# First Q and K in full precision from unsplit weights, x split once with its sums in place, two gate pairs interleaved, weight sums as additions

## The chip, the core and the metric

The kernel runs on one core of one Trainium2 chip. The metric is the device time of one execution in microseconds (us): 1400.05 before, the median of three runs (1399.22 to 1400.08). TensorE (PE) multiplies matrices and adds into PSUM; VectorE (DVE), ScalarE (ACT) and GpSimd (POOL) work on tiles; SyncE (SP) issues most transfers.

## What is computed

One hybrid layer in fp32 for 512 tokens of width 2048: an RMS norm, one input projection, three attention branches of four heads of 128 columns, merge gates, and an output projection with the residual.

```python
hn = rmsnorm(x, norm_g)
proj = jnp.einsum('bsd,dc->bsc', hn, w_in)
br = proj[..., :QKVG_COLS].reshape(b, s, N_BRANCH, 4, BRANCH_W)       # q, k, v, g
f_logit = proj[..., QKVG_COLS:QKVG_COLS + N_HEADS] + b_f
gates = jax.nn.sigmoid(proj[..., QKVG_COLS + N_HEADS:] + b_gate).reshape(b, s, N_BRANCH, D_MODEL)
...
ys = ys * jax.nn.silu(br[:, :, :, 3])
up = jnp.einsum('bsnw,nwd->bsnd', ys, w_up)
merged = jnp.sum(gates * up, axis=2)
return x + jnp.einsum('bsd,de->bse', merged, w_out)
```

## The kernel before

Branch A is an attention with forget gates (four logits per token, the "four heads' logits"), B a chunked one with a learned bias, C a stick-breaking one. The kernel takes the branches in the order C, B, A, four heads each, then the up projections with the merge gates, then the output projection.

**Three products for one.** A factor in fp32 is split into a high and a low part of type fp32r: ACT rounds the high part (`split_to`, L92), VectorE subtracts it from the tile for the low part (L93). `mm3` multiplies high by high, low by high and high by low (L101 to L103), so one matmul is three rows. Weights arrive as raw tiles of 512 KB (`load`, L138: six slots), and are split into `wh` and `wl` (three slots each). x lies transposed, 16 k tiles of 128 by 512 tokens, multiplied by the norm's gain; `rstd`, the norm's factor of each token, is known only after the sums of squares (`norm_x`, L247) and `rsqrt` (L235 to L240).

**Pairs.** `pair_task` computes two column tiles of 128 with seven products in place of eight (Strassen's scheme in Winograd's form): a product has 24 rows of 256 tokens. It needs sums of the weights' four blocks (raw tiles added on VectorE: L315, L324, L325, L327) and of x (`combos`: x by gain and rstd on VectorE, L255, four sums on GpSimd, L257 to L260, and their splits). The results come together in three tiles u, c1, c2 (`after_of`). Both gate pairs that follow the first head, all heads but the first, the other gates and the output projection go by pairs. The first head's Q, K, V and G (`first_head`) go by whole columns (`col_task`, 512 tokens, two units of 24 rows), from x without rstd, which is multiplied in as they leave PSUM (`scaled`, L626); x is split then (`prep_x`), and again after the norm for the pairs (`parts1`, `parts2`).

**The order.** The work is a list of units of up to 24 matmul rows. The emission at the end of the program splits the weights of a unit three units ahead and loads them seven ahead; `at` hangs further work, such as the stages of a head's attention (`stick_scores`, `stick_sums` L548, `soft_scores`, `av`), on a later unit by the numbers in `OFF`. For the first `OFF["man"]` units PE keeps the order of the code; from then on a scheduler orders each engine's instructions when the program is built. PSUM has four banks `acc` for products and four `att` for all else.

## Time and profile before

| what | value |
| --- | --- |
| runs, median of three | 1400.05 us (1399.22 to 1400.08) |
| profiled execution: span | 1397.6 us |
| PE busy, share of the span | 98% |
| VectorE, ACT, GpSimd busy | 85%, 52%, 4% |
| transfers, mean | 126 GB/s |

The profile is of one execution; its span lies 2.45 us under the median of the runs. In a line of the timeline stand the start, the length, the engine, the line of the kernel, the tile written and the tiles read, and in brackets the idle time ahead with what ended it. Matmul rows overlap, so what one costs is the distance of two starts, not its length.

### The profile page before, as it was taken

How to read it: one execution, taken by the hardware profiler on the slowest of the kernel's cores; microseconds unless marked ns; L12 is line 12 of the kernel's file. 1: busy time of each engine (PE TensorE's matmuls, PEld its weight loads, DVE VectorE, ACT ScalarE, POOL GpSimd, SP SyncE). 2: the span in 40 equal slices, each digit the busy share in tenths (PEclk: the TensorE clock that was granted, in tenths of full speed). 3: DMA queues.
4: the chain of work that ended last, by engine and by line, in shares of the span. 5: the costliest groups of instructions: out<-in, count | busy, mean ns of one | idle time of the engine just before them, and what ended most of it. 6: DMA issues, size and time to landing. Idle time of an engine off the chain costs nothing.

```text
span 1397.6 us, 25474 instructions
## 1 busy us (share of the span) xinstructions
PE 1366.3 (98%) x10452; PEld 1316.7 (94%) x10452; DVE 1191.8 (85%) x1671; ACT 729.7 (52%) x1042; POOL 53.7 (4%) x60
## 2 busy tenths in 40 slices
PE   6969999999999999999999999999999999999999
PEld 3759999999999999999999999999999988899999
DVE  8999898887978889888888888888888888898886
ACT  6345564544545555555556555545555755453332
POOL 4730000000000000000000000000000000000000
PEclk9989999999999999999999999999999999999999
DMA  7113334323344244342433333333233766535542
GB/s 272 46 46 106 122 102 126 121 91 114 106 129 126 95 114 128 113 129 95 117 122 115 121 94 119 113 114 121 91 115 103 273 197 203 169 109 176 164 151 76
DMA packets 63093, 176.39 MB, mean 126 GB/s; under 512 B 7400, under 2 KB 9320, under 8 KB 62976
## 3 DMA queue, kind: packets, MB, share of 16 engines
q1 hardware_dynamic: 59520, 170.49, 38.4%
q10 hardware_dynamic: 3456, 4.26, 0.8%
q8 instruction: 82, 1.34, 0.4%
q14 instruction: 35, 0.29, 0.1%
HBM read 155.04 MB, written 19.69 MB: 125 GB/s over the span
## 4 chain that ended last, share of the span: by engine, by line
PE 92%; DVE 5%; issue 1%; ACT 0%; POOL 0%; DMA 0%; SPq 0%; DVEq 0%; ACTq 0%; POOLq 0%
PE acc L101 27%; PE acc L103 27%; PE acc L102 27%; PE att L103 3%; PE att L101 3%; PE att L102 3%; DVE x L255 1%; DVE wl L93 1%; PE att L548 1%; PE att L517 1%; PE att L570 1%; DVE x1l L93 1%; PE att L571 1%; PE att L569 1%; DVE t23l L93 0%
## 5 line engine op out<-in xcount | busy, mean ns | idle before, releaser
L92 ACT ACTIVATE wh<-raw 128x1024 fp32r<-128x1024 f32 (+1 forms) x418 | 435.7, 1043 | 549.2 <-PE acc L102 488.2
L93 DVE TENSOR_TENSOR wl<-raw,wh 128x1024 fp32r<-128x1024 f32 (+1 forms) x418 | 503.9, 1206 | 96.7 <-ACT wh L92 95.9
L102 PE MATMUL acc<-x1l,wh 128*128 128x256 f32 (+1 forms) x768 | 222.3, 289 | 10.5 <-DVE x1l L93 10.5
L103 PE MATMUL acc<-x1h,wl 128*128 128x256 f32 (+1 forms) x768 | 222.0, 289 | 2.2 <-DVE wl L93 2.2
L101 PE MATMUL acc<-x1h,wh 128*128 128x256 f32 (+1 forms) x768 | 223.7, 291 | 0.0
L101 PE MATMUL acc<-x2h,wh 128*128 128x256 f32 (+1 forms) x768 | 223.6, 291 | 0.0
L102 PE MATMUL acc<-x2l,wh 128*128 128x256 f32 (+1 forms) x768 | 221.9, 289 | 0.9 <-DVE x2l L93 0.9
L103 PE MATMUL acc<-x2h,wl 128*128 128x256 f32 (+1 forms) x768 | 221.8, 289 | 0.0
L101 PE MATMUL acc<-t23h,wh 128*128 128x256 f32 x736 | 209.7, 285 | 0.0
L103 PE MATMUL acc<-t23h,wl 128*128 128x256 f32 x736 | 208.4, 284 | 0.0
L102 PE MATMUL acc<-t23l,wh 128*128 128x256 f32 x736 | 208.1, 283 | 0.0
L102 PEld LDWEIGHTS acc<-x1l,wh 128*128 128x128 f32 x768 | 147.8, 192 | 13.4 <-DVE x1l L93 11.2
L103 PEld LDWEIGHTS acc<-x1h,wl 128*128 128x128 f32 x768 | 147.8, 193 | 3.9 <-DVE wl L93 2.4
L102 PEld LDWEIGHTS acc<-x2l,wh 128*128 128x128 f32 x768 | 148.0, 193 | 2.4 <-DVE x2l L93 1.1
L101 PEld LDWEIGHTS acc<-x1h,wh 128*128 128x128 f32 x768 | 147.9, 193 | 1.8 <-issue 0.2
L101 PEld LDWEIGHTS acc<-x2h,wh 128*128 128x128 f32 x768 | 148.2, 193 | 1.3
L103 PEld LDWEIGHTS acc<-x2h,wl 128*128 128x128 f32 x768 | 148.0, 193 | 1.3
L101 PEld LDWEIGHTS acc<-t23h,wh 128*128 128x128 f32 x736 | 141.0, 192 | 0.5
L102 PEld LDWEIGHTS acc<-t23l,wh 128*128 128x128 f32 x736 | 141.0, 192 | 0.1
L103 PEld LDWEIGHTS acc<-t23h,wl 128*128 128x128 f32 x736 | 140.7, 191 | 0.3
L101 PE MATMUL acc<-t,wh 128*128 128x256 f32 x368 | 105.1, 286 | 0.0
L102 PE MATMUL acc<-t,wh 128*128 128x256 f32 x368 | 104.4, 284 | 0.0
(256 smaller groups left out, 2728.0 us busy)
## 6 DMA issues: line engine op xcount, KB each, us to landing
raw<-in_w_col SPq DMA_DIRECT2D x192, 512.0 KB, 3.6
raw<-in_w_out SPq DMA_DIRECT2D x32, 512.0 KB, 3.8
gl<-c SPq DMA_DIRECT2D x48, 256.0 KB, 2.0
raw<-in_w_up SPq DMA_DIRECT2D x32, 384.0 KB, 3.2
sg<-gl SPq DMA_DIRECT2D x48, 256.0 KB, 5.0
x<-in_xT SPq DMA_DIRECT2D x16, 256.0 KB, 5.4
xr<-in_xT SPq DMA_DIRECT2D x16, 256.0 KB, 4.4
yd<-y SPq DMA_DIRECT2D x11, 256.0 KB, 2.0
```

Of the source, the lines that this page charges most:

```text
L92: nc.scalar.activation(hi, src, AF.Copy)
L93: nc.vector.tensor_sub(lo, src, f(hi))
L101: nc.tensor.matmul(ps, lh, rh, start=start, stop=False)
L102: nc.tensor.matmul(ps, lh, rl, start=False, stop=False)
L103: nc.tensor.matmul(ps, ll, rh, start=False, stop=stop)
L255: nc.vector.scalar_tensor_tensor(x, x, gn[:, kt:kt + 1], rstd[0], op0=ALU.mult, op1=ALU.mult)
L517: nc.tensor.transpose(ps[:, blk(i)], st["p"][i][:, blk(j)], identf)
L548: nc.tensor.matmul(ps[:, i * P:], nu_r if i == j else nones_r, part, start=i == j and part is st["lk"][j][0], stop=False)
L569: nc.tensor.matmul(o, vh[:, blk(j)], st["h"][j], start=j == 0, stop=False)
L570: nc.tensor.matmul(o, vl[:, blk(j)], st["h"][j], start=False, stop=False)
L571: nc.tensor.matmul(o, vh[:, blk(j)], st["l"][j], start=False, stop=j == QB - 1)
```

## The change

The first head's Q and K are computed by `first_pair`: 32 fp32 matmuls of the raw weights with x, which ACT multiplies by its gain in place; the norm's sums stand after k tile 9. Then x is multiplied by rstd in place and split once (`split_x`), and V and G go by that; they leave PSUM as copies on ACT (`kept`). The sums of x are made in place on VectorE (`combos`), and their signs turned, which turns signs in `after_of` and `merged_combos`. The four heads' logits follow V and G. The two gate pairs behind them are `late`: their units alternate, one of each pair, and their weight sums are made by transfers that GpSimd issues and that add to the tile (`load_of`). The same holds for the first pair of the output projection, without alternation. In all other pairs VectorE adds, product 5 comes first, and product 3 is added into product 5's bank of PSUM (`more`), to which the last line of `mms_of` belongs. Lines of after lie some ten below or above those of before: the splits are still L92 and L93, the rows of `mm3` L102 to L104.

```diff
-    def mm3(ps, lh, ll, rh, rl, start, stop):
-        nc.tensor.matmul(ps, lh, rh, start=start, stop=False)
-        nc.tensor.matmul(ps, lh, rl, start=False, stop=False)
-        nc.tensor.matmul(ps, ll, rh, start=False, stop=stop)
+    def mm3(ps, lh, ll, rh, rl, start, stop, more=False):
+        nc.tensor.matmul(ps, lh, rh, start=start, stop=False, skip_group_check=more)
+        nc.tensor.matmul(ps, lh, rl, start=False, stop=False, skip_group_check=more)
+        nc.tensor.matmul(ps, ll, rh, start=False, stop=stop, skip_group_check=more)
...
     def prep_x(kt):
         x = xraw[kt]
-        h, lo = xs[kt]
-        if kt % 2:
-            nc.vector.tensor_scalar_mul(h, x, gn[:, kt:kt + 1])
-        else:
-            nc.scalar.activation(h, x, AF.Copy, scale=gn[:, kt:kt + 1])
-        nc.vector.scalar_tensor_tensor(lo, x, gn[:, kt:kt + 1], f(h), op0=ALU.mult, op1=ALU.subtract)
-        s = sqp[kt // 2 % 2] if kt % 2 and kt > 1 else t2("sq")
+        s = t2("sq")
         nc.scalar.activation(s, x, AF.Square)
+        nc.scalar.activation(x, x, AF.Copy, scale=gn[:, kt:kt + 1])
         if kt < 2:
             ssq[kt] = s
         else:
-            (nc.gpsimd, nc.vector)[kt % 2].tensor_add(ssq[kt % 2], ssq[kt % 2], s)
+            nc.vector.tensor_add(ssq[kt % 2], ssq[kt % 2], s)
...
+    def split_x(kt):
+        nc.vector.tensor_mul(xraw[kt], xraw[kt], rstd[0])
+        split_to(*xs[kt], xraw[kt])
     def combos(k):
         a, b = xraw[k], xraw[k + UK]
-        for x, kt in ((a, k), (b, k + UK)):
-            nc.vector.scalar_tensor_tensor(x, x, gn[:, kt:kt + 1], rstd[0], op0=ALU.mult, op1=ALU.mult)
-        t, u = t2("t23"), t2("t4")
-        nc.gpsimd.tensor_sub(t[:, RH], b[:, RH], a[:, RH])
-        nc.gpsimd.tensor_sub(a[:, RH], a[:, RH], a[:, LH])
-        nc.gpsimd.tensor_sub(t[:, LH], b[:, RH], a[:, RH])
-        nc.gpsimd.tensor_sub(u[:, LH], t[:, LH], b[:, LH])
-        split_to(*t23[k], t)
-        split_to(t4[k][:, LH], t4[k][:, RH], u[:, LH])
+        nc.vector.tensor_sub(a[:, LH], a[:, LH], a[:, RH])
+        nc.vector.tensor_sub(a[:, RH], b[:, RH], a[:, RH])
+        nc.vector.tensor_add(b[:, RH], b[:, RH], a[:, LH])
+        nc.vector.tensor_sub(b[:, LH], b[:, RH], b[:, LH])
+    def split_t1(k):
+        (h, lo), a = x1[k], xraw[k]
+        split_to(h[:, RH], lo[:, RH], a[:, LH])
+    def split_t(k):
+        (h, lo), a, b = t23[k], xraw[k], xraw[k + UK]
+        split_to(h[:, LH], lo[:, LH], b[:, RH])
+        split_to(h[:, RH], lo[:, RH], a[:, RH])
+        split_to(t4[k][:, LH], t4[k][:, RH], b[:, LH])
...
-        order = (1, 2, 5, 3, 6, 7, 4) if late else (1, 2, 6, 7, 4, 5, 3)
+        order = (1, 2, 3, 5, 6, 7, 4) if late else (5, 1, 2, 6, 7, 4, 3)
+        (a11, a12), (a21, a22) = src1, src2
+        parts = {1: [a11], 2: [a12], 4: [a22], 5: [a21, a22], 7: [a11, a21], 6: [a21, a22, a11],
+                 3: [a21, a22, a11, a12]}
+        def load_of(i):
+            def go(u):
+                if late:
+                    p = order[i]
+                    w[p] = raw_tile()
+                    nc.sync.dma_start(w[p], parts[p][0])
+                    for src in parts[p][1:]:
+                        nc.gpsimd.dma_start(w[p], src, accum_op=ALU.add)
+                elif i == 0:
+                    for p, src in ((7, a21), (4, a22), (1, a11), (2, a12)):
+                        w[p] = raw_tile()
+                        nc.sync.dma_start(w[p], src)
+            return go
         def prep_of(i):
             p = order[i]
             def go(u):
-                if i == 0:
-                    w[1], a21, w[4], w[2] = kept
-                    split_to(u.hi, u.lo, w[1])
+                if not late and p == 5:
                     w[5] = raw_tile()
-                    nc.vector.tensor_add(w[5], a21, w[4])
-                    if late:
-                        nc.vector.tensor_sub(a21, w[1], a21)
-                        nc.vector.tensor_sub(w[1], w[5], w[1])
-                    w[7], w[6], w[3] = a21, w[1], w[2]
-                    return
+                    nc.vector.tensor_add(w[5], w[7], w[4])
                 split_to(u.hi, u.lo, w[p])
-                if i == 1:
-                    if not late:
-                        nc.vector.tensor_sub(w[7], w[1], w[7])
-                        nc.vector.tensor_sub(w[6], w[5], w[1])
-                if i == (1 if late else 4):
-                    nc.vector.tensor_sub(w[3], w[3], w[6])
+                if not late and p == 1:
+                    w[6] = w[5]
+                    nc.vector.tensor_add(w[7], w[7], w[1])
+                    nc.vector.tensor_add(w[6], w[6], w[1])
+                elif not late and p == 6:
+                    w[3] = w[6]
+                    nc.vector.tensor_add(w[3], w[3], w[2])
             return go
         def mms_of(i):
+            p = order[i]
             def go(u):
-                st["ps"] = ps = acc()[:, LH]
+                more = p == 3 and not late
+                st[p] = ps = st[5] if more else acc()[:, LH]
                 for j in range(UK):
-                    mm3(ps, u.hi[:, j, :], u.lo[:, j, :], *ops[order[i]](j), j == 0, j == UK - 1)
+                    mm3(ps, u.hi[:, j, :], u.lo[:, j, :], *ops[p](j), j == 0 and not more, j == UK - 1, more)
...
-                    add(u[:, LH], u[:, LH], ps)
+                    sub(u[:, LH], ps, u[:, LH])
                     if late:
-                        add(c1[:, RH], c1[:, RH], u[:, LH])
+                        sub(c1[:, RH], c1[:, RH], u[:, LH])
                 elif p == 7:
-                    add(u[:, RH], u[:, LH], ps)
-                    if late:
-                        add(c2[:, RH], c2[:, RH], u[:, RH])
+                    sub(u[:, RH], u[:, LH], ps)
+                    sub(c2[:, RH], u[:, RH], c2[:, RH] if late else st[5])
                 elif p == 4:
                     sub(c2[:, LH], u[:, RH], ps)
                 elif p == 5 and late:
                     nc.scalar.activation(c2[:, RH], ps, AF.Copy)
-                elif p == 5:
-                    add(c2[:, RH], u[:, RH], ps)
-                    add(u[:, LH], u[:, LH], ps)
-                elif late:
-                    add(c1[:, RH], c2[:, RH], ps)
-                else:
-                    add(c1[:, RH], u[:, LH], ps)
+                    add(c1[:, RH], c1[:, RH], ps)
+                elif p == 3 and late:
+                    nc.scalar.activation(c1[:, RH], ps, AF.Copy)
+                elif p == 3:
+                    sub(c1[:, RH], ps, u[:, LH])
...
-    def scaled(st, r):
+    def first_pair(st, n, h):
+        cols = {r: col(n, r, h) for r in (Q, K)}
+        raw = {}
+        ps = {r: Lazy(acc) for r in cols}
+        def load(u):
+            def w(r, i, a, b):
+                if (r, i) not in raw:
+                    raw[r, i] = raw_tile()
+                nc.sync.dma_start(raw[r, i][:, a:b, :], cols[r][i][:, a:b, :])
+            h4 = UK // 2
+            load_x(0)
+            w(Q, 0, 0, h4)
+            w(K, 0, 0, h4)
+            for kt in range(1, UK):
+                load_x(kt)
+            w(Q, 0, h4, UK)
+            w(K, 0, h4, UK)
+            for kt in range(UK, KT):
+                load_x(kt)
+            for r in cols:
+                w(r, 1, 0, UK)
+        def mms(u):
+            for kt in range(KT):
+                for r in cols:
+                    nc.tensor.matmul(ps[r](), raw[r, kt // UK][:, kt % UK, :], xraw[kt],
+                                     start=kt == 0, stop=kt == KT - 1)
+                if kt == OFF["ssq"]:
+                    with tc.high_priority():
+                        norm_x()
+        def after():
+            for kt in range(KT):
+                split_x(kt)
+            for r in cols:
+                st[r] = t2("c")
+                nc.vector.tensor_mul(st[r], ps[r](), rstd[0])
+        return Unit(None, None, mms, load=load, after=after)
+    def kept(st, r):
         def evac(ps):
             st[r] = t2("c")
-            nc.vector.tensor_mul(st[r], ps, rstd[0])
+            nc.scalar.activation(st[r], ps, AF.Copy)
         return evac
     def first_head(n, h):
         st = {}
         fu, fps = f_units()
-        c = {r: col_task(col(n, r, h), xs, scaled(st, r)) for r in (Q, K, V, G)}
-        units.extend([fu[0], c[Q][0], c[K][0], fu[1], c[Q][1], c[K][1],
-                      c[V][0], c[G][0], c[V][1], c[G][1]])
-        def norm_first():
-            with tc.high_priority():
-                norm_x()
-        at(1, norm_first)
-        for k in range(UK):
-            at(OFF["c0"] + k // OFF["c1"], lambda k=k: combos(k))
+        c = {r: col_task(col(n, r, h), xs, kept(st, r)) for r in (V, G)}
+        units.extend([first_pair(st, n, h), c[V][0], c[G][0], c[V][1], c[G][1], fu[0], fu[1]])
+        pairs = []
+        for _ in range(2):
+            u0 = len(units)
+            gate_units(late=True)
+            pairs.append(units[u0:])
+            del units[u0:]
+        units.extend(u for two in zip(*pairs) for u in two)
+        def sums():
+            for k in range(UK):
+                combos(k)
         def parts1():
             for k in range(UK):
-                split_to(*x1[k], xraw[k])
+                split_t1(k)
         def parts2():
             for k in range(UK):
-                split_to(*x2[k], xraw[k + UK])
+                split_t(k)
+        def forget():
             v = t2("f")[:2 * NH, :]
-            nc.vector.tensor_mul(v, fps[:2 * NH, :], rstd[0][:2 * NH, :])
+            nc.scalar.activation(v, fps[:2 * NH, :], AF.Copy)
             nc.sync.dma_start(fd, v)
-            at(12, forget_bias)
-        at(7, parts1)
-        at(9, parts2)
+            at(OFF["fb"], forget_bias)
+        at(OFF["tf"], sums)
+        at(5, parts1)
+        at(6, forget)
+        at(7, parts2)
...
-        gate_units(late=OFF["l1"])
-        gate_units(late=OFF["l2"])
...
-    prep_to(1)
-    load_to(2)
-    for kt in range(4, 8):
-        load_x(kt)
-    load_to(3)
-    for kt in range(8, KT):
-        load_x(kt)
-    for kt in range(UK):
+    load_to(1)
+    for kt in range(KT):
         prep_x(kt)
-    prep_to(2)
-    for kt in range(UK, KT):
-        prep_x(kt)
-        if kt == 11:
-            prep_to(3)
+    load_to(4)
...
-OFF = dict(cs=4, ct=12, nk=5, nq=4, s=12, t=16, v=1, av=8, a0=11, b0=18, c0=3, c1=2, man=17, last=3, l1=0, l2=0)
+OFF = dict(tf=2, cs=4, ct=12, nk=5, nq=4, s=12, t=16, v=1, av=8, ssq=9, fb=10, a0=8, b0=15, man=14, last=3)
```

**GpSimd, in the gate pairs.** Before, its rows are the sums of x, four for each of eight k tiles (t23 and t4 are the sums' tiles); two k tiles:

```order
L257 TENSOR_TENSOR t23_109_427<-x_71_213,x_1_81 128x256
L258 TENSOR_TENSOR x_1_81<-x_1_81 128x256
L259 TENSOR_TENSOR t23_109_427<-x_71_213,x_1_81 128x256
L260 TENSOR_TENSOR t4_110_428<-t23_109_427,x_71_213 128x256
L257 TENSOR_TENSOR t23_111_439<-x_72_215,x_2_83 128x256
L258 TENSOR_TENSOR x_2_83<-x_2_83 128x256
```

After, its rows there are the adding transfers; the last number of a tile tells the product (566 is product 3 of the first pair, 607 of the second; 635 and 719 product 5, 763 and 806 product 6, 862 and 895 product 7):

```order
L322 DMA raw_126_566<-in_w_col 128x1024 x3
L322 DMA raw_129_607<-in_w_col 128x1024 x2
L322 DMA raw_133_635<-in_w_col 128x1024
L322 DMA raw_129_607<-in_w_col 128x1024
L322 DMA raw_140_719<-in_w_col 128x1024
L322 DMA raw_151_763<-in_w_col 128x1024 x2
L322 DMA raw_164_806<-in_w_col 128x1024
L322 DMA raw_168_862<-in_w_col 128x1024
L322 DMA raw_164_806<-in_w_col 128x1024
L322 DMA raw_172_895<-in_w_col 128x1024
```

The sums of x have gone to VectorE, and GpSimd's queue holds ten groups of transfers, in which one tile's transfers stand apart (607, 806).

**VectorE, behind the norm.** Before, the rows behind rstd are the 16 products with gain and rstd, L255; the splits of x by the norm follow later. After, L231 makes rstd, and 13 scalings of k tiles of x (x_59 to x_73) follow it; the last two of them, and what stands behind:

```order
L244 TENSOR_TENSOR x_72_219<-x_72_219,rstd_106_338 128x512
L244 TENSOR_TENSOR x_73_221<-x_73_221,rstd_106_338 128x512
L93 TENSOR_TENSOR x1l_11_138<-x_59_191,x1h_10_137 128x512
L93 TENSOR_TENSOR x1l_13_140<-x_62_197,x1h_12_139 128x512
L93 TENSOR_TENSOR x1l_15_142<-x_63_199,x1h_14_141 128x512
L244 TENSOR_TENSOR x_74_223<-x_74_223,rstd_106_338 128x512
L93 TENSOR_TENSOR x1l_17_144<-x_64_201,x1h_16_143 128x512
```

The first low part now stands behind 13 of the 16 scalings.

**ACT, at the sums of a stick-breaking head (the second of branch C).** Before, between the last exponent of lk and the next evacuation:

```order
L535 ACTIVATE lk_326_1897<-lk_326_1897 128x512
L92 ACTIVATE wh_345_2011<-raw_318_1818 128x1024
L92 ACTIVATE lkh_291_1654<-lk_321_1852 128x384
L92 ACTIVATE lkh_290_1653<-lk_326_1897 128x512
L347 ACTIVATE u_330_1934<-acc_329_1909 128x256
L92 ACTIVATE wh_348_2041<-raw_301_1669 128x1024
```

After:

```order
L550 ACTIVATE lk_309_1840<-lk_309_1840 128x512
L92 ACTIVATE wh_328_1953<-raw_283_1610 128x1024
L92 ACTIVATE wh_331_1983<-raw_302_1761 128x1024
L92 ACTIVATE lkh_275_1598<-lk_305_1796 128x384
L92 ACTIVATE lkh_274_1597<-lk_309_1840 128x512
L366 ACTIVATE u_313_1877<-acc_324_1897 128x256
```

A second weight split now stands ahead of both splits of lk. On PE the row that reads the last of them comes right behind the end of the unit in acc_330:

```order
L102 MATMUL acc_330_1957<-t23h_40_167,wh_318_1884 128x256
L103 MATMUL acc_330_1957<-t23l_41_168,wh_318_1884 128x256
L104 MATMUL acc_330_1957<-t23h_40_167,wl_319_1885 128x256
L563 MATMUL att_340_2020<-lkh_274_1597,nu_r_97 128x512
```

More of the change, by code (lines that the diff above doesn't have):

```diff
@@ L124, in hybrid_kernel, with __init__ @@
     class Unit:
-        def __init__(self, shape, prep, mms, srcs=(), after=None):
-            self.shape, self.prep, self.mms, self.srcs, self.after = shape, prep, mms, srcs, after
+        def __init__(self, shape, prep, mms, src=None, load=None, after=None):
+            self.shape, self.prep, self.mms, self.src, self.load, self.after = shape, prep, mms, src, load, after
             self.hi = self.lo = None
@@ L134, in load @@
     def load(u):
-        u.raw = []
-        for s, keep in u.srcs:
-            t = raw_tile(u.shape)
-            nc.sync.dma_start(t, s)
-            u.raw.append(t)
-            if keep is not None:
-                keep.append(t)
+        if u.load is not None:
+            u.load(u)
+        elif u.src is not None:
+            u.raw = raw_tile(u.shape)
+            nc.sync.dma_start(u.raw, u.src)
     def prep(u):
-        if u.shape is None:
+        if u.prep is None:
             return
@@ L150, in prep_raw @@
     def prep_raw(u):
-        split_to(u.hi, u.lo, u.raw[0])
-    for kt in range(4):
-        load_x(kt)
+        split_to(u.hi, u.lo, u.raw)
     epsc = cp.tile([P, 1], F32, name="epsc")
@@ L340, in go @@
             def go():
-                ps = st["ps"]
+                ps = st[p]
                 if i == 0:
@@ L373, in after_of @@
             return go
-        src = {0: [(src1[0], kept), (src2[0], kept), (src2[1], kept), (src1[1], kept)]}
-        return [Unit([UK, P], prep_of(i), mms_of(i), srcs=src.get(i, ()), after=after_of(i)) for i in range(7)]
+        return [Unit([UK, P], prep_of(i), mms_of(i), load=load_of(i), after=after_of(i)) for i in range(7)]
     side = {}
@@ L744, in after @@
                 merged_combos(d - UK, last_m[0], m)
-        return [Unit([6, P], prep_raw, mms(i), srcs=[(w_up[d, i], None)], after=after if i == 1 else None)
+        return [Unit([6, P], prep_raw, mms(i), src=w_up[d, i], after=after if i == 1 else None)
                 for i in range(2)]
@@ L759, in merged_combos @@
         nc.vector.tensor_sub(t[:, RH], b[:, RH], a[:, RH])
[L760 to L761 removed]
+        nc.vector.tensor_sub(a[:, RH], a[:, LH], a[:, RH])
+        nc.vector.tensor_add(t[:, LH], b[:, RH], a[:, RH])
         nc.vector.tensor_sub(u, t[:, LH], b[:, LH])
@@ L795, in hybrid_kernel, with rest @@
     for e in range(0, DT, 2):
-        def rest(c1l, c1r, c2, e=e):
-            for c, i, sl in ((c2, 1, slice(0, S)), (c1l, 0, LH), (c1r, 0, RH)):
+        def rest(c1l, v, c2, e=e):
+            for c, i, sl in ((c2, 1, slice(0, S)), (c1l, 0, LH), (v, 0, RH)):
                 if i == 1 or sl is LH:
@@ L800, in rest @@
                     nc.sync.dma_start(r, xT[e + i])
-                nc.vector.tensor_add(c, c, r[:, sl])
+                (nc.vector.tensor_sub if sl is RH else nc.vector.tensor_add)(c, c, r[:, sl])
             nc.scalar.dma_start(out[e + 1], c2)
```

7 lines of the change are left out of this document (1 added, 6 removed).

## The prediction

> **What bounds the kernel now.** I read the engine shares first, then the span cut at the places where TensorE stops, then the neighbourhood of each stop.
>
> ```profile
> span 1397.6 us, 25474 instructions
> PE 1366.3 (98%) x10452; PEld 1316.7 (94%) x10452; DVE 1191.8 (85%) x1671; ACT 729.7 (52%) x1042; POOL 53.7 (4%) x60
> ```
>
> The windows, with each engine's busy time in them:
>
> ```profile
> core 0: us, PE busy (x) PEld busy (x) DVE busy (x) ACT busy (x) POOL busy (x), PEclk, DMA share, GB/s
> 0.00:20.16 20.16, 7.74 (x16) 1.15 (x16) 16.05 (x28) 12.40 (x19) 11.20 (x23) 1.00 0.94 350
> 20.16:25.60 5.44, 5.44 (x13) 4.25 (x14) 5.44 (x8) 4.87 (x8) 2.49 (x2) 1.00 0.64 256
> 25.60:72.07 46.47, 46.47 (x202) 35.88 (x200) 44.17 (x52) 17.59 (x28) 27.44 (x24) 1.00 0.19 58
> 72.07:95.02 22.95, 9.34 (x47) 8.22 (x46) 22.95 (x28) 11.44 (x20) 11.05 (x10) 0.70 0.01 1
> 95.02:1237.00 1141.98, 1141.98 (x8894) 1112.88 (x8895) 972.48 (x1387) 621.12 (x895) 1.51 (x3) 1.00 0.40 125
> 1237.00:1262.00 25.00, 22.98 (x186) 22.17 (x185) 23.77 (x36) 13.91 (x23) 0.00 (x0) 1.00 0.34 110
> ```
>
> TensorE (PE) is full for 1141.98 us on end. It idles in three places only: ahead of 20.16, in 72.07 to 95.02, where VectorE (DVE) is busy all the time, and by 2.02 in 1237 to 1262 (what is left of the end is the last stores). So an edit counts by the matmul rows it adds or takes, and by what it does at those places; VectorE's 85% counts nowhere else unless PE comes to wait for it.
>
> **Q and K in full precision.**
>
> ```profile
> 26.10 0.39 PE L103 MATMUL acc<-x1h,wl 128*128 128x512 f32 x1
> 26.33 0.39 PE L101 MATMUL acc<-x1h,wh 128*128 128x512 f32 x1
> ```
>
> and the first rows of the norm, which are fp32:
>
> ```profile
> 28.37 1.02 PE L247 MATMUL att<-sq,tmpc 128*128 128x512 f32 x2
> ```
>
> Split rows of 512 columns start 0.227 apart. The norm's fp32 matmul takes two rows, 0.43 apart (1.02 less 0.59, the length of one), so 0.86. 32 x 0.86 = 27.5 for 96 x 0.227 = 21.8: **+5.7**.
>
> **The start.**
>
> ```profile
> 20.16 0.59 PE L399 MATMUL att<-x1l,w 128*8 128x512 f32 x1 [3.28 <-DVE x1l L224]
> 20.55 0.63 PE L101 MATMUL acc<-x1h,wh 128*128 128x512 f32 x1
> 20.97 0.63 PE L102 MATMUL acc<-x1l,wh 128*128 128x512 f32 x1
> ```
>
> Those were PE's rows in time order; ACT's first square, and its squares and scalings grouped:
>
> ```profile
> 6.02 0.60 ACT L226 ACTIVATE att<-x 128x512 f32<-128x512 f32 x1 [1.26 <-DMA x<-in_xT]
> L226 ACT ACTIVATE sq<-x x9: 612/612/631, 9.5 to 23.9; 128x512 f32<-128x512 f32 x9
> L223 ACT ACTIVATE x1h<-x,small_in x4: 702/706/722, 4.0 to 11.6; 128x512 fp32r<-128x512 f32 x4
> ```
>
> Dense work begins at 20.16, with 15 rows (3.4 us of work) done: 16.8 lost. After, the first product needs only x0 at its gain, behind four squares on ACT. The fourth square reads x3, which now is the sixth 256 KB transfer, not the fourth: at 350 GB/s 0.75 later each, so about 7.5; a square and a scaling (0.61, 0.71) make 8.9: **-7.9**. Rows start 0.42 apart for the first 5.4 us here; I take the same loss for the new start.
>
> **The norm and the split of x.**
>
> ```profile
> 30.47 0.69 ACT L235 ACTIVATE rt<-att,epsc 128x512 f32<-128x512 f32 x1 [0.46 <-PE att L247]
> 34.61 0.69 DVE L240 SCALAR_TENSOR_TENSOR rstd<-rw,rt 128x512 f32<-128x512 f32 x1
> 91.02 1.87 DVE L93 TENSOR_TENSOR x2l<-x,x2h 128x512 fp32r<-128x512 f32 x3
> 188.06 1.06 ACT L92 ACTIVATE wh<-raw 128x1024 fp32r<-128x1024 f32 x1
> 93.16 1.21 DVE L93 TENSOR_TENSOR wl<-raw,wh 128x1024 fp32r<-128x1024 f32 x1
> ```
>
> In ACT's new order three weight splits stand among the last five squares; their load, behind 6.3 MB at 350 GB/s, lands near 22. From there 3 splits, 3 squares and 4 scalings, then VectorE's low part (1.2) and two sums, end near 31.9; PE reaches the norm rows after k tile 9 at 8.9 + 2.7 + 20 x 0.86 = 28.8, and waits about 3.2. The rows end at 33.7; rstd takes from about 30.4 to 35.3 in the rows above, 4.9, so it is there at 38.6. PE has 12 fp32 matmuls left and comes to V at 44.0. VectorE's order is 13 scalings by rstd, then eight low parts, with three scalings and one eviction among them: (1.87 - 0.67) / 2 = 0.60 each, 25 x 0.61 = 15.3. V's first half needs them one by one and ends at 54.2 rather than 44.0 + 24 x 0.227 = 49.4: 4.8. Together **+8.0**; between 0 (squares early, low parts ahead of PE) and 12.8 (the splits' load 4.8 later, by the slowest landing below).
>
> **The gap at 72 to 95.**
>
> ```profile
> 74.65 0.39 PE L103 MATMUL acc<-x1h,wl 128*128 128x256 f32 x1 [2.19 <-DVE wl L93]
> 81.47 0.58 PE L102 MATMUL acc<-x1l,wh 128*128 128x256 f32 x1 [4.18 <-DVE x1l L93]
> 88.75 0.58 PE L102 MATMUL acc<-x1l,wh 128*128 128x256 f32 x1 [6.27 <-DVE x1l L93]
> 95.24 0.28 PE L103 MATMUL acc<-x2h,wl 128*128 128x256 f32 x1
> 95.36 0.28 PE L101 MATMUL acc<-t23h,wh 128*128 128x256 f32 x1
> ```
>
> VectorE's low parts beside GpSimd (54 to 84; busy, mean ns) and then without it (least, median, most ns):
>
> ```profile
> L93 DVE TENSOR_TENSOR x1l<-x,x1h 128x512 fp32r<-128x512 f32 x7 | 8.2, 1221 | 0.0
> ```
>
> ```profile
> L93 DVE TENSOR_TENSOR x2l<-x,x2h x8: 670/674/683, 84.1 to 94.3; 128x512 fp32r<-128x512 f32 x8
> ```
>
> PE waits for the second split of x, which VectorE does late: beside GpSimd's sums (busy 27.44 and 11.05 in the two windows) a low part takes 1.22, without them 0.67. After, x is split once, the sums stand on VectorE at its free pace, the four heads' logits and both gate pairs' products that need no sums lie ahead of those that do. The 47 rows there need 47 x 0.12 = 5.6: 22.95 - 5.6, **-17.3**. What is late next is the sums T2, T3, T4, due only with product 6; I expect them in time.
>
> **Stick-breaking heads.**
>
> ```profile
> 189.07 1.05 ACT L92 ACTIVATE lkh<-lk 128x384 fp32r<-128x384 f32 x2
> ...
> 190.94 1.06 ACT L92 ACTIVATE wh<-raw 128x1024 fp32r<-128x1024 f32 x1 [0.55 <-PE acc L102]
> ```
>
> Before, the weight split that awaits the end of a unit (last row) stands behind the splits of lk that the sums on PE read. After, in heads 1 to 3 of branch C, it stands ahead of two of them, and the next PE row is the sum that reads them. The weight split's slot comes free only as that unit ends, so PE waits 1.06 + 1.05 = 2.1, three times: **+6.2**. Low end 0, if the unit ends earlier than ACT comes to it.
>
> **Accumulating transfers.** 21 weight sums are added by transfers issued on GpSimd, 14 in the gate pairs, 7 in the first output pair. No row of before has such a transfer; the nearest is the plain 512 KB load:
>
> ```profile
> raw<-in_w_col SPq DMA_DIRECT2D x192, 512.0 KB, 3.6
> ```
>
> ```profile
> L138 SPq DMA_DIRECT2D raw<-in_w_col x192: 327/328/780, 2.7 to 1060.8; - x192
> ...
> DMA to landing us min/median/max: 2.8/3.6/8.4
> ```
>
> GpSimd takes them in order and each needs the one before on its tile. Product 3 of the second pair gets its slot when G's second half is split, so its plain load lands near 67. From there five links follow in series to the second product 6 (two of product 3, two of product 6 and the load or sum between), with three issues by GpSimd among them, which I put at 0.6 to 1 each, an estimate from the 0.33 to 0.78 that SyncE's issues of the same tiles take. PE wants that product at 54.2 + 3 x 5.45 (V, G) + 7.3 (logits, 32 rows of 0.227) + 9 x 2.88 (products of 24 rows of 0.12) + 1.0 of narrow starts = 104.8, its split 1.2 earlier. So the chain is late if a link exceeds (103.6 - 67 - 3) / 5 = 6.7. Ends: 2.8, a plain load's least, and 10.5, the slowest plain load with a quarter on top. A sum reads its source and the tile it adds to, twice what a load reads: 2 x 3.6 = 7.2; the slowest load was 8.4, and 7.8 stands between. I take it: 5 x 1.1 = **+5.5**. The first output pair has three such links in series to its product:
>
> ```profile
> 1239.05 0.38 PE L101 MATMUL acc<-m2h,wh 128*128 128x256 f32 x1 [0.37 <-ACT wh L92]
> ...
> 1240.31 0.39 PE L103 MATMUL acc<-m2h,wl 128*128 128x256 f32 x1 [0.76 <-DVE wl L93]
> ```
>
> 3 x 1.1 = **+3.3**, beside the waits that stand there already. Each us on a link is worth 8.
>
> At nothing I cost the copies of V and G on ACT (52% busy), the turned signs, and two weight sums fewer on VectorE per pair where it has slack; if that cover failed, a copy would cost 0.6, four heads' worth 2.4. Adding product 3 into product 5's bank makes PE wait for VectorE's read of that bank after product 7; product 4's 24 rows (2.88) stand between and hide one read of 0.4.
>
> **Sum.** 5.7 - 7.9 + 8.0 - 17.3 + 6.2 + 5.5 + 3.3 = +3.5. The profiled execution's span is 1397.6, the median of the runs shown 1400.05, 2.45 more. So 1401.1 + 2.45, **1403.6**. What a measurement of this kernel can tell from no change is 0.2%, so the same is 1397.25 to 1402.85.
>
> **Rivals.** (a) The other side, **faster**: a link lands in 7.0 or less. At 6.7 the 5.5 and 3.3 are gone, and it is 1394.7, 5.3 under before. For it: the median load of 3.6, and the transfer engines at share 0.19 and 0.01 from 25.6 to 95. Against: a sum is two reads and a write, in series, from an engine that issues none now. At 8 us for each us of link a gain ends at 6.7 + 5.3 / 8 = 7.4, and one that can be measured (2.8) at 7.0. The Trainium skill, "DMA: Bandwidth & Descriptors", section "Anatomy of one DMA — SWDGE (gpsimd) path", fits GpSimd's transfers as 2.0 us and bytes at 436 GB/s, 3.2 here, by which this rival would hold; no run here shows it, and the plain load from SyncE took 3.6.
>
> (b) **Links of 10.5** or more: 2.7 more on eight, 1425.
>
> (c) **VectorE holds up GpSimd's issues.** The rows of 1.22 against 0.67 show the two in each other's way. If each link loses one more such pair (1.2), 8 x 1.2 = +9.6, 1413. Against: the issue moves no data through GpSimd's own datapath that this trace shows. The Trainium skill, "SBUF — State Buffer", section "SBUF: two separate sides", warns that GpSimd cannot write a transfer's descriptors while VectorE runs an operation in a two-port mode, and elsewhere on the page it infers that an addition of two tiles doesn't block that; the slowed rows here are additions of two tiles against GpSimd's arithmetic, so they don't settle it.
>
> (d) **Each pair waits for the bank** by a weight split's length, 50 x 1.2 = 60 more, 1464, if VectorE's queue puts the read behind others; it decides from 2.88.
>
> (e) **No stick-breaking waits:** 6.2 less, 1397.4.
>
> **Chances.** Forecast 0.42 (links of 7.0 to 8.7; own range 1397 to 1411), (a) 0.30, (c) 0.08, (b) 0.09, (e) 0.06, (d) 0.03, and 0.02 for none. Faster: 0.30 of (a), 0.02 of (e), 0.02 for none, 0.34. Same: 0.20 of the forecast, 0.04 of (e), 0.24. Slower: 0.22 of the forecast, (b), (c) and (d), 0.42. Range 1390 to 1426: from (a) with half the norm's term gone, to (b).
>
> **What would show it.** PE's first product near 9; a wait ahead of the norm's rows; waits for x1l up to 54; no idle stretch at 72 to 95; three waits of 2.1 at the stick-breaking sums for lkh; landing times of GpSimd's transfers, and PE waiting for a weight's high part near 105 and 1240. It is wrong if a link takes under 7.0 or over 8.7, if PE waits at each product 3, or if the sums T2 to T4 come late and PE idles in the gates as before.

## The result, and the profile after

The changed kernel takes 1411.84 us, the median of four runs (1411.17 to 1412.49), where the kernel before took 1400.07 beside it (1399.22 to 1400.96): a ratio of 1.0084 [1.0070, 1.0098], so slower by 11.8. The forecast was 1403.6, with 1390 to 1426 as its range. The profiled execution's span is 1410.0, 12.4 more than before and 8.9 more than the forecast's 1401.1.

The page of the changed kernel begins so:

```profile
span 1410.0 us, 25473 instructions
PE 1374.5 (97%) x10420; PEld 1315.0 (93%) x10420; DVE 1142.8 (81%) x1632; ACT 733.0 (52%) x1070; POOL 22.6 (2%) x42
```

TensorE has 32 rows fewer than before and yet is busy 8.2 us longer. Rows that take longer than they should show in the granted clock, so the next view is the windows, cut where TensorE's waits end; columns as before (busy time and instructions of each engine, then clock, share of the transfer engines, GB/s):

```profile
core 0: us, PE busy (x) PEld busy (x) DVE busy (x) ACT busy (x) POOL busy (x), PEclk, DMA share, GB/s
0.00:9.86 9.86, 0.00 (x0) 0.00 (x0) 3.00 (x13) 4.46 (x7) 2.74 (x18) 1.00 0.81 262
9.86:52.65 42.79, 38.26 (x93) 17.77 (x94) 28.47 (x45) 29.88 (x50) 1.01 (x1) 1.00 0.63 212
52.65:92.48 39.83, 35.63 (x203) 28.05 (x201) 33.34 (x80) 22.03 (x48) 7.99 (x10) 0.99 0.79 173
92.48:95.40 2.92, 2.92 (x13) 2.92 (x14) 2.92 (x6) 0.00 (x0) 0.65 (x1) 0.50 1.00 171
95.40:113.37 17.97, 14.70 (x119) 14.22 (x117) 7.50 (x26) 5.51 (x13) 2.59 (x3) 0.97 1.01 263
113.37:119.40 6.03, 5.56 (x24) 5.27 (x25) 5.93 (x10) 4.08 (x9) 0.00 (x0) 0.50 0.62 203
119.40:1237.00 1117.60, 1111.71 (x8623) 1082.53 (x8622) 924.39 (x1279) 599.55 (x866) 4.97 (x7) 1.00 0.39 126
1237.00:1262.00 25.00, 21.30 (x152) 20.25 (x151) 19.36 (x30) 14.68 (x26) 2.62 (x3) 0.93 0.82 216
```

And what TensorE waited for (total, times, longest):

```profile
engine line waited for: us in total, times, longest us
PE acc L665 <- DMA x<-in_xT: 9.9, 1, 9.9
PE att L563 <- ACT lkh L92: 5.9, 3, 2.0
PE acc L104 <- DVE wl L93: 4.9, 3, 4.2
PE acc L102 <- ACT m2h L92: 3.5, 1, 3.5
PE acc L102 <- ACT wh L92: 3.3, 1, 3.3
PE acc L103 <- DVE x1l L93: 2.6, 3, 2.1
PE att L238 <- DVE sq L221: 1.7, 1, 1.7
```

The stretch of 72 to 95 in which TensorE idled for 13.6 is gone, and V's first half ends at 52.65. In its place stand waits at 92.48 (4.2), at 113.37 (3.28, and 0.47 at the third row), three of 1.96 at the stick-breaking sums (L563), and 3.70 of idleness in 1237 to 1262, 1.68 more than before. Behind most of them the clock is at a half (0.50 in two windows above), and rows of 256 columns start 0.21 apart instead of 0.12.

The wait at 113.37 is the chain of adding transfers that the prediction foresaw, at product 6 of the second pair. The one at 92.48 it did not foresee. TensorE's rows at it, and VectorE's of the same time:

```profile
88.00 0.28 PE L103 MATMUL acc<-x2l,wh 128*128 128x256 f32 x1
92.48 0.58 PE L104 MATMUL acc<-x2h,wl 128*128 128x256 f32 x1 [4.20 <-DVE wl L93]
...
90.72 0.24 DVE L429 SCALAR_TENSOR_TENSOR lf<-lf,small_in 128x16 f32<-128x16 f32 x1 [6.49 <-DMA lf<-fd]
...
91.21 1.22 DVE L93 TENSOR_TENSOR wl<-raw,wh 128x1024 fp32r<-128x1024 f32 x1
```

VectorE stands idle for 6.49, waiting for the four heads' logits to come back from memory (lf from fd), and the low part `wl` of product 3 is queued behind. SyncE's issues of that store and of the first of two reloads:

```profile
77.19 0.34 SPq L714 DMA_DIRECT2D fd<-f  x1
82.33 0.35 SPq L427 DMA_DIRECT2D lf<-fd  x1
```

The two loads of 8 KB take from 82.3 to 90.7, 8.4 us; before, that tile's landed in 1.7 in the median. They run among the adding transfers, for which the page and the answer for their line have:

```profile
raw<-in_w_col POOLq DMA_DIRECT2D x14, 512.0 KB, 7.7
...
DMA to landing us min/median/max: 5.3/8.5/11.8
```

A link, one adding transfer from issue to landing, takes 7.7 in the gate pairs' median and 8.5 over all 21, between 5.3 and 11.8.

### The profile page after: what moved, and what is told of

The parts are those of the page before. It is cut to its first block, busy times and chain, and to the rows that moved or that the text cites. A ratio compares the mean times of both kernels' runs of the same rounds, so it can differ in the third digit from the quotient of the medians.

```text
span 1410.0 us, 25473 instructions
## 1 busy us (share of the span) xinstructions
PE 1374.5 (97%) x10420; PEld 1315.0 (93%) x10420; DVE 1142.8 (81%) x1632; ACT 733.0 (52%) x1070; POOL 22.6 (2%) x42
## 3 DMA queue, kind: packets, MB, share of 16 engines
q0 software_dynamic: 3024, 11.01, 4.3%
## 4 chain that ended last, share of the span: by engine, by line
PE 90%; DMA 5%; DVE 3%; ACT 1%; issue 1%; POOL 0%; SPq 0%; DVEq 0%; ACTq 0%; POOLq 0%
PE acc L104 26%; PE acc L102 26%; PE acc L103 26%; PE att L102 2%; PE att L104 2%; PE att L103 2%; DMA raw<-in_w_out 2%; DMA raw<-in_w_col 2%; PE att L563 1%; DVE wl L93 1%; DMA x<-in_xT 1%; DVE x L244 1%; PE att L532 1%; ACT wh L92 1%; DMA lf<-fd 1%
## 5 line engine op out<-in xcount | busy, mean ns | idle before, releaser
L92 ACT ACTIVATE wh<-raw 128x1024 fp32r<-128x1024 f32 (+1 forms) x414 | 430.6, 1043 | 552.6 <-PE acc L103 443.8
L93 DVE TENSOR_TENSOR wl<-raw,wh 128x1024 fp32r<-128x1024 f32 (+1 forms) x414 | 495.2, 1200 | 107.1 <-ACT wh L92 105.3
L104 PE MATMUL acc<-x2h,wl 128*128 128x256 f32 (+1 forms) x752 | 215.5, 287 | 4.2 <-DVE wl L93 4.2
L103 PE MATMUL acc<-x1l,wh 128*128 128x256 f32 (+1 forms) x752 | 215.2, 286 | 2.8 <-DVE x1l L93 2.6
L102 PE MATMUL acc<-x1h,wh 128*128 128x256 f32 (+1 forms) x752 | 217.0, 289 | 0.0
L102 PE MATMUL acc<-x2h,wh 128*128 128x256 f32 (+1 forms) x752 | 216.0, 287 | 0.0
L102 PE MATMUL acc<-t23h,wh 128*128 128x256 f32 x736 | 212.6, 289 | 3.3 <-ACT wh L92 3.3
L103 PE MATMUL acc<-x2l,wh 128*128 128x256 f32 (+1 forms) x752 | 215.6, 287 | 0.0
L104 PE MATMUL acc<-x1h,wl 128*128 128x256 f32 (+1 forms) x752 | 215.3, 287 | 0.0
L104 PE MATMUL acc<-t23h,wl 128*128 128x256 f32 x736 | 210.8, 286 | 0.5 <-DVE wl L93 0.5
L104 PEld LDWEIGHTS acc<-x2h,wl 128*128 128x128 f32 x752 | 144.9, 193 | 5.0 <-DVE wl L93 4.4
L102 PEld LDWEIGHTS acc<-t23h,wh 128*128 128x128 f32 x736 | 143.7, 195 | 4.1 <-ACT wh L92 3.7
L102 PEld LDWEIGHTS acc<-x2h,wh 128*128 128x128 f32 x752 | 144.9, 193 | 0.7
L102 PEld LDWEIGHTS acc<-x1h,wh 128*128 128x128 f32 x752 | 144.0, 191 | 1.6 <-ACT x1h L92 0.2
L104 PEld LDWEIGHTS acc<-x1h,wl 128*128 128x128 f32 x752 | 143.9, 192 | 0.6
L104 PEld LDWEIGHTS acc<-t23h,wl 128*128 128x128 f32 x736 | 143.5, 195 | 0.8 <-DVE wl L93 0.8
L102 PE MATMUL acc<-t,wh 128*128 128x256 f32 x368 | 105.5, 287 | 0.0
L104 PE MATMUL acc<-t,wl 128*128 128x256 f32 x368 | 104.2, 283 | 0.0
```

The source lines that it names most:

```text
L92: nc.scalar.activation(hi, src, AF.Copy)
L93: nc.vector.tensor_sub(lo, src, f(hi))
L102: nc.tensor.matmul(ps, lh, rh, start=start, stop=False, skip_group_check=more)
L103: nc.tensor.matmul(ps, lh, rl, start=False, stop=False, skip_group_check=more)
L104: nc.tensor.matmul(ps, ll, rh, start=False, stop=stop, skip_group_check=more)
```

## The experiments

Each is the changed kernel with the edit shown, unless said otherwise. The changed kernel was measured again for the comparison (e10, "the repeat"); its median was then 1410.02 (1407.83 to 1411.41), ratio 1.0070 [1.0057, 1.0082], so that 1 to 2 us between two medians say little, and the traces decide there.

**The forget logits later** (e1; in `forget`, bias and reload behind the last product of the second pair).

```diff
-            nc.sync.dma_start(fd, v)
-            at(OFF["fb"], forget_bias)
+            def later():
+                z = sp.tile([P, 1], F32, tag="small", name=nm("zb"))
+                nc.vector.tensor_scalar_mul(z, late_c[-1][:, :1], 0.0)
+                nc.scalar.activation(v, v, AF.Identity, bias=z[:2 * NH, :])
+                nc.sync.dma_start(fd, v)
+                at(cur[0] + 4, forget_bias)
+            at(20, later)
```

> The four heads' logits go to memory and come back only after the two gate pairs, by an operand that waits for the second pair; all else as in the change (1411.8). Theory A, the reload holds VectorE's queue, where product 3's low part stands behind it, and with it GpSimd's next transfer: the wait of 4.2 at 92 goes with its slow rows (1.4), the transfers behind it move up by some 6, and most of the wait of 3.75 at 113 with its slow rows (3.0) goes: 8 to 12 less, 1400 to 1404. Theory B, the links of 7.7 are the bound and the reload is incidental: product 3 waits as long for its own transfers, at most 2 less, 1410 or more.

Measured: 1409.73, ratio 1.0068 [1.0051, 1.0084], 2 less than the changed kernel and 0.3 less than its repeat. The wait at 92 is gone, so the reload was its cause, as theory A has it; but the next one grew from 3.28 to 4.97 (with 0.46 behind it, 5.43), and the gain that theory A expected did not come. GpSimd's rows there:

```profile
78.21 2.62 POOL L322 DMA_DIRECT2D raw<-in_w_col  x3 [4.14 <-DMA raw<-in_w_col]
91.95 2.65 POOL L322 DMA_DIRECT2D raw<-in_w_col  x3 [11.12 <-DMA raw<-in_w_col]
```

Of three transfers issued from 78.21 on, one lands only at 91.95; the chain of links sets the end, not TensorE's start of it. The two waits are in series on TensorE and both end by things that run on meanwhile, so taking the first away lengthens the second. How they share the time changes from one execution to the next: in the repeat, the same program, VectorE waited 3.30 for the reload, and TensorE waited little at product 3 and long at product 6:

```profile
88.75 0.39 PE L104 MATMUL acc<-x2h,wl 128*128 128x256 f32 x1 [1.03 <-DVE wl L93]
111.31 0.58 PE L102 MATMUL acc<-t23h,wh 128*128 128x256 f32 x1 [6.24 <-ACT wh L92]
```

With 0.46 behind the second that is 7.73, where the first trace has 4.20 + 3.28 + 0.47 = 7.95: the sum stays, the parts do not.

**The output pair's sums on VectorE** (e2), **the gates' sums on VectorE and one pair behind the other** (e4). In both, the four raw tiles come by plain loads and the same additions are made as in all other pairs; e4 also takes the alternation out.

```diff
+                if late and adds and p == 1:
+                    w[5] = raw_tile()
+                    nc.vector.tensor_add(w[5], w[7], w[4])
+                    nc.vector.tensor_add(w[7], w[7], w[1])
+                    w[6] = w[1]
+                    nc.vector.tensor_add(w[6], w[5], w[1])
+                elif late and adds and p == 2:
+                    w[3] = w[2]
+                    nc.vector.tensor_add(w[3], w[6], w[2])
...
-        units.extend(u for two in zip(*pairs) for u in two)
+        units.extend(u for one in pairs for u in one)
```

> First output pair with its weight sums as additions on VectorE and plain loads from SyncE, order of products kept; all else as in the change (1411.8). Theory A, ACT stands at a weight split that awaits an adding transfer, and the split of the merged rows behind it is late for that: the wait of 3.55 at 1247 goes, 3 to 4 less, 1408 to 1409. Theory B, the merged rows themselves come late: within 1 of 1411.8, with the wait still on the split of the merged rows.

> The two late gate pairs one after the other, with their weight sums as additions on VectorE and no adding transfers in them; the output pair keeps its transfers; all else as in the change (1411.8). Theory A, the adding transfers and what they crowd cost the gates their waits (8.0 of idle and 4.4 of slow rows): 9 to 13 less, 1399 to 1403. Theory B, without the interleaving the sums of x are late for the first product 6, 5.8 us earlier in the order: a new wait of 4 or more on their low parts, 1405 to 1410.

Measured: e2 1408.43, ratio 1.0057 [1.0042, 1.0072], and the wait of 3.55 before m2h is gone (0.49 and 0.76 are left there). In the changed kernel ACT had stood 5.77 at a weight split that awaited an adding transfer, with the split into m2h next in its order:

```profile
1245.99 1.06 ACT L92 ACTIVATE wh<-raw 128x1024 fp32r<-128x1024 f32 x1 [5.77 <-DMA raw<-in_w_out]
1246.95 0.61 ACT L92 ACTIVATE m2h<-m 128x512 fp32r<-128x512 f32 x1
```

e4 measured 1404.15, ratio 1.0024 [1.0014, 1.0033], 6 to 8 less than the changed kernel, between the two theories. Its two edits were not tried one by one. Of the gates' waits e4 keeps one, with another cause, VectorE being busy throughout (27.00 of 27.00 us in 59 to 86):

```profile
85.46 0.39 PE L104 MATMUL acc<-x2h,wl 128*128 128x256 f32 x1 [3.30 <-DVE wl L93]
```

**Product 3's split behind the stick-breaking splits** (e3): on ACT the last split of lk and the copy of product 1's bank go ahead of the weight split.

```diff
+                with ExitStack() as behind:
+                    if not late and p == 3:
+                        for ins in first.values():
+                            behind.enter_context(tc.issue_after(ins.ins))
+                    split_to(u.hi, u.lo, w[p])
```

> The weight split of product 3 is put behind the splits of lk and behind the copy of product 1 in ACT's order, nothing else; in the change 1411.8. Theory A, that split's wait for a unit's end holds up the rows that PE reads next: the three waits of 1.96 fall to at most 1, and the half-speed rows behind two of them go: 6 to 9 less, 1403 to 1406. Theory B, VectorE's masks of lk are late (they end at 190.8 where PE's unit ends at 190.2): waits of 1.5 or more stay, and at most 2 go, 1410.

Measured: 1403.16, ratio 1.0015 [1.0006, 1.0024], 7 to 9 less. One wait of 1.06 is left in the first of the three heads, no half clock behind any:

```profile
192.91 0.50 PE L570 MATMUL att<-lkh,nu_r 128*128 128x512 f32 x1 [1.06 <-ACT lkh L559]
```

So the order of ACT's queue was the cause, and the price was more than the 5.9 of waiting.

**No adding transfers** (e5), **plain ones in their place** (e6): one line is taken out, or loses its addition.

```diff
-                        nc.gpsimd.dma_start(w[p], src, accum_op=ALU.add)
+                        nc.gpsimd.dma_start(w[p], src)
```

> The change without its 21 adding transfers: their weight sums hold only their first part, so those pairs' products are of other weights; every other instruction stays. Theory A, the adding transfers load the transfer engines so that they and all else in 60 to 110 wait (share 0.9 and more at 204 GB/s): the share there falls below 0.6, the reload of the logits lands in 4 rather than 8.4, and the waits at 92 and 113 in the gates and at 1247 all but go: 9 to 14 less than 1411.8. Theory B, VectorE's queue and the reload set the wait at 92: a wait of 3 or more stays there.

> The change with the same 21 transfers issued by GpSimd, as plain loads that overwrite the tile instead of adding to it, so those sums hold only their last part; waits and order stay. Theory A, the addition is what is slow: landing near SyncE's 3.7, at most 5, more GB/s at less share, and waits as without the transfers, 1398 to 1403. Theory B, GpSimd's way of issuing is slow (descriptors, or VectorE in its way): landing stays at 7 or more and the time near 1411.8.

Measured, one run each: 1393.78 and 1397.14, some 4 and 1 below the ranges of their theories A. Windows of the gate pairs in the changed kernel, in e5 and in e6 (the columns of the windows view):

```profile
60.00:90.00 30.00, 28.29 (x171) 21.96 (x169) 24.23 (x61) 19.43 (x45) 5.33 (x7) 1.00 0.91 204
90.00:115.00 25.00, 18.77 (x133) 18.01 (x134) 13.78 (x35) 7.14 (x16) 4.32 (x5) 0.88 0.89 220
```

```profile
60.00:90.00 30.00, 30.00 (x187) 23.84 (x185) 29.88 (x71) 19.54 (x46) 0.00 (x0) 1.00 0.36 108
90.00:115.00 25.00, 25.00 (x207) 24.86 (x206) 20.63 (x47) 15.23 (x27) 0.00 (x0) 1.00 0.54 170
```

```profile
60.00:90.00 30.00, 30.00 (x188) 23.87 (x186) 29.89 (x71) 19.44 (x45) 4.30 (x9) 1.00 0.69 235
90.00:115.00 25.00, 25.00 (x207) 24.86 (x206) 20.64 (x48) 15.46 (x29) 1.52 (x3) 1.00 0.72 249
```

e6 has the same 21 transfers from the same queue, in the same series, beside the same work of VectorE. TensorE never idles, and the bytes move at 235 and 249 GB/s with the transfer engines at 0.69 and 0.72; with the addition it is 204 and 220 at 0.91 and 0.89. The answers for their landing in e6:

```profile
raw<-in_w_col POOLq DMA_DIRECT2D x14, 512.0 KB, 4.7
...
DMA to landing us min/median/max: 3.7/5.5/8.5
```

So it is the addition that makes a link 7.7 instead of 4.7 and fills the transfer engines, and neither GpSimd's queue nor VectorE's work beside it. The packets of that queue, 3024 and 11.01 MB in both, took 4.3% of the transfer engines' time with the addition and 2.3% without. And in e6 VectorE used the reloaded logits 2.8 after the reload's issue, without a wait, where it was 8.4 among adding transfers.

**All three mends together** (e7: e2, e3 and e4), **and the splits of the sums of x behind the waiting low part as well** (e8: in `parts2`, from the fourth k tile on).

> All weight sums as additions on VectorE (gate pairs one after the other, output pair too), and product 3's split put behind the splits of lk: the three edits of before together. If their gains add (3.4, 7.7 and 8.7 of 1411.8): 1392, faster than before by 8. If they share a cause, 1397 or more. Expected waits: the start, 0.8 to 2 at the norm, 2.1 at x's low part, 3.3 at product 3 of the first gate pair.

> As the kernel with all three edits, and VectorE's splits of the sums of x from the fourth k tile on stand behind the low part of product 3's weights. Theory A, the wait of 3.3 at product 3 is only VectorE's order: it falls to 1.5 or less and no other appears, 2 to 3 less. Theory B, VectorE is the bound from 59 to 96: what is moved behind is late at product 6, and the time is within 1 of the kernel with three edits.

Measured: e7 **1390.25** (1389.92 to 1392.06), ratio 0.9935 [0.9920, 0.9950]; e8 1391.79, ratio 0.9940 [0.9924, 0.9957]. e7 is faster than both kernels, by 9.6 than the one before; its gain over the changed kernel, 21.6, is near the 19.8 that the three single gains add up to. In e8 the wait of 3.33 shrinks to 1.47, but two new ones come at later products, and the time is no better. The first (0.91) is for a low part, with VectorE busy 11.00 of 11.00 us in 85 to 96, so there what is moved back is late next; the second (2.05) ends with a copy on ACT, and its cause is not shown.

**Extra rows while TensorE waits** (e9, and e11 at another place), beside **the changed kernel again** (e10). In the three heads eight rows are issued ahead of the sums, into the bank that the sums' first row then overwrites.

```diff
+                if j == 0 and h > 0:
+                    with tc.issue_after(tail["mm"].ins):
+                        for _ in range(8):
+                            nc.tensor.matmul(ps, nones_r, xs[0][0], start=True, stop=True)
```

> After the change TensorE waits 1.96 us at the sums of each of three stick-breaking heads; behind two of the three its rows run at half clock for a stretch that costs 1.7. Here eight rows more (8 x 0.227 = 1.8 us, into the same bank of att, overwritten by the sums' first row) stand on TensorE between the end of the unit and the sums, so that it is busy while it would wait; nothing else is changed. Theory A: idling brings the half clock. Then the sums start when they did, what is left of each wait is under 0.5, no half-clock rows follow in any of the three heads, and the kernel is 3.4 us faster than after the change (between 1.7 and 5.1, as one to three stretches are avoided): 1408.4, 1406.7 to 1410.2. Theory B: the half clock has another cause there, the rows themselves or the transfers beside them: the stretches stay in most heads and the time is 1411.8, or up to 1 more where a row too many delays the sums.

> The changed kernel once more, for a second trace of the same program. Theory A, that a half-clock stretch follows an idle stretch or not by when it falls: the waits stay as they were within 0.3 us, but which of the three heads' waits is followed by half-clock rows differs, and the time lies within 1409 to 1414. Theory B, that it is settled by the program: the first head's wait is followed by none and the other two by a stretch each, as before.

e9 measured 1415.49, ratio 1.0115 [1.0100, 1.0131], and tells nothing of the clock's cause: its order came out otherwise. TensorE ran the next unit ahead of the sums, waited at that unit's start 2.23 for a copy on ACT that stood behind the same splits, and the extra rows came where nothing waited, 3 x 1.8 = 5.4 more than the repeat, about their whole length. e11 pins them to the end of the unit before (`tail["end"]` for `tail["mm"]`), and ACT's order is that of the changed kernel.

> The eight extra rows of the run before the last (e9) again, now right behind the end of the unit at which TensorE waits after the change, with ACT's order as after the change (both weight splits, both splits of lk, the copy u). TensorE is then busy 1.8 of the 1.96 us that it waits in each of three heads. Theory A, idling brings the half clock: what is left of the three waits is under 0.5 each, none of the three heads shows half-clock rows within 6 us behind (by chance alone, as behind 7 of 21 such waits, that would be one in 27), and the sums start when they did, so a stretch of 1.7 is saved for each that would have come: 0 to 5.1, most likely 3.4, off the 1410.0 to 1411.8 of the two measurements after the change; 1407.5. Theory B, the half clock comes from the rows or the transfers there: stretches in one to three of the heads all the same, and 1410 to 1412.

Measured: 1409.61, ratio 1.0067 [1.0053, 1.0081], the repeat's time. The same 15 us around the three heads' sums, in the changed kernel, in its repeat and in e11:

```profile
186.00:201.00 15.00, 13.04 (x108) 12.74 (x107) 14.34 (x22) 7.38 (x14) 0.00 (x0) 1.00 0.33 107
276.00:291.00 15.00, 13.04 (x95) 12.74 (x94) 12.45 (x20) 5.84 (x11) 0.00 (x0) 0.89 0.29 106
368.00:383.00 15.00, 13.04 (x95) 12.75 (x94) 12.78 (x21) 7.00 (x13) 0.00 (x0) 0.89 0.34 106
```

```profile
185.00:200.00 15.00, 13.04 (x108) 12.74 (x107) 14.34 (x23) 7.38 (x14) 0.00 (x0) 1.00 0.33 107
275.00:290.00 15.00, 13.04 (x95) 12.74 (x95) 12.47 (x21) 5.54 (x10) 0.00 (x0) 0.89 0.32 106
367.00:382.00 15.00, 13.04 (x108) 12.75 (x107) 14.28 (x23) 7.52 (x12) 0.00 (x0) 1.00 0.34 106
```

```profile
182.00:197.00 15.00, 15.00 (x119) 14.59 (x118) 13.69 (x21) 9.07 (x15) 0.00 (x0) 1.00 0.39 124
272.00:287.00 15.00, 15.00 (x119) 14.58 (x118) 13.72 (x21) 8.74 (x15) 0.00 (x0) 1.00 0.40 124
364.00:379.00 15.00, 15.00 (x119) 14.58 (x118) 13.93 (x21) 7.68 (x14) 0.00 (x0) 1.00 0.33 107
```

TensorE idles 1.96 in each of the first six windows (15.00 less 13.04). Where the clock reads 0.89 it did 95 rows, where it reads 1.00 it did 108: a stretch at half clock costs 0.11 x 15 = 1.65. Which heads have one differs between the two traces of the same program, so it isn't settled by the program. With TensorE kept busy there is none in any of the three. That is as theory A has it, and by chance one in 27; the time does not show it, since with one stretch in the repeat's trace the gain to expect is about 1.65, and the repeat's own runs lie up to 3.6 apart. So idling as the cause rests on traces, not on a time: on those of e11 and e3, and on the sorting of all waits by the clock's windows in the last section.

## Why the prediction came out as it did

The sign of the result, slower, was the forecast's (0.42), and the time lies in its outer range, but 8 above its own value and just above the 1397 to 1411 that it gave that forecast. Its terms against the trace of after:

**Q and K, start and norm (5.7, -7.9, 8.0)** were right together: V's first half ends at 52.65, where 54.2 was expected. In single terms there were errors of 1 to 1.5 that in part cancel: the first product came at 9.86, not 8.9; the wait ahead of the norm's rows was 1.73, not 3.2; and the last fp32 rows, 24 in 9.90 (32.62 to 42.52), are 0.41 apart, not 0.43:

```profile
30.83 1.96 PE L238 MATMUL att<-sq,tmpc 128*128 128x512 f32 x4 [1.73 <-DVE sq L221]
32.62 10.46 PE L665 MATMUL acc<-x,raw 128*128 128x512 f32 x24
42.52 0.79 PE L102 MATMUL acc<-x1h,wh 128*128 128x512 f32 x1
```

**The gap (-17.3)** was right: nothing of the waits for the second split of x is left.

**The accumulating transfers in the gates (5.5)**: the link was estimated at 7.8 and measured 7.7 (7.4 in the repeat); with the reload out of the way (e1) the chain's waits were 5.43. In the changed kernel itself the waits in the gates are 4.20 + 3.28 + 0.47 = 7.95, 2.45 more, because the step that gave VectorE's queue no transfer to wait for was incomplete: it counted the links and their issues, and left out that the logits' reload, on which VectorE waits in order, shares the transfer engines with them. The repeat's 7.73 says the same of the sum.

**Stick-breaking heads (6.2)**: the waits were 5.9. **The output pair (3.3)**: 1.68 of idleness, and not where it was expected: TensorE waited for m2h, which stood behind the late weight split on ACT, not for its own weights.

**What was missing** is a term for the clock. After a wait the forecast let TensorE go on at full speed. From the windows above, the loss is the length times what the clock lacks: 0.50 x 2.92 and 0.50 x (6.03 - 0.47) in the gates, 4.2; two of 1.65 at the heads, 3.3; 0.07 x 25 at the output pair, 1.75; in all 9.3. With it the account closes: -1.55 (V earlier), +2.45 (gates), -0.3 (heads), -1.6 (output pair), +9.3 make 8.3 of the 8.9; the rest is small waits for x1l and wl. The row for it was in the prediction's own table: the gap of before stood at a granted clock of 0.70, and it was read as part of a gap that goes, not as what any new wait would bring with it. Without these 9.3 the change would have been some 2.5 slower, less than the 2.8 that the prediction called measurable. So that it came out clearly slower rests on a cost that the forecast did not have, and the right sign is in part luck.

**The rivals.** (a) falls: a link of 7.0 or less was the condition, and it took 7.7 and 8.5. (b) falls, since 10.5 was reached by single transfers only. (c), VectorE holding up GpSimd's issues, falls by e6, where VectorE's rows are the same and the plain transfers keep up, and by the issues' own length, 0.85 in the least and 0.86 in the median of 14; the time came near its 1413 for another reason. (d) falls: no wait for product 5's bank stands among TensorE's waits. (e) falls with three waits of 1.96. The Trainium skill's fit of GpSimd's transfers ("DMA: Bandwidth & Descriptors", section "Anatomy of one DMA — SWDGE (gpsimd) path"), by which 3.2 was worked out, fits neither the adding transfers here (7.7) nor the plain ones of e6 (4.7), which both ran beside other transfers.

## What to carry to other kernels

A new wait of 2 us on TensorE is to be priced at its length and a likely stretch at half clock behind it (1.65 here, behind 14 of 21 such waits). An addition done by a transfer is not free because its engine idles: ask what share of the transfer engines it takes, and which small transfer on another engine's path runs among them. Of waits in series, take away what bounds the chain: without the reload, but with the chain, the gain was 0.3 to 2; without the chain's transfers and the alternation it was 6 to 8.
